# A decoder step on one core: the attention stage in another order of steps, with softmax scaling and weight splits on other engines

## The chip, the cores and the metric

The kernel runs on one core of a Trainium2 chip. The metric is the device time of one execution in microseconds (us). A core has five engines that matter here, each with its own in-order queue of instructions: TensorE (PE in the profile), VectorE (DVE), ScalarE (ACT), GpSimd (POOL) and SyncE (SP), which here only issues transfers. An instruction waits on semaphores for what other engines or transfers deliver, and whatever stands behind it on its engine waits too.

## The reference, cut to what matters

One layer of a decoder trunk runs over 256 prompt tokens and 8 samples of 4 new tokens, 288 columns in all. A first projection gives inputs of a recurrent branch, queries, three sets of keys and values, and gates; both branches are merged by gated projections; a convolutional feed-forward block follows. The changed stage computes the attention branch:

```python
def masked_softmax(s, mask):
    s = jnp.where(mask, s.astype(jnp.float32), NEG)
    e = jnp.where(mask, jnp.exp(s - jnp.max(s, axis=-1, keepdims=True)), 0.0)
    return e / jnp.maximum(jnp.sum(e, axis=-1, keepdims=True), 1e-30)
...
    g = jax.nn.sigmoid(g_nsa).reshape(B, T, 3, N_KV, HPG, 1)
    o = (g[:, :, 0] * o_cmp + g[:, :, 1] * o_slc + g[:, :, 2] * o_win).reshape(B, T, D_ATT)
    m = (jax.nn.sigmoid(g_m[..., :D_MODEL]) * (y_rnn @ w_proj_rnn)
         + jax.nn.sigmoid(g_m[..., D_MODEL:]) * (o @ w_proj_att))
```

There are three attentions (compressed, selected, window) over 8 heads in 2 groups. For the 256 prompt tokens all keys are on the chip; for each of the 8 samples 256 old keys and values of the selected and of the window branch come from memory. The kernel multiplies the gate of a branch into its softmax.

## The kernel before

All activations lie transposed, features on the 128 partitions and the 288 tokens along the free axis. Every weight product is made of three fp32r products (`mm3`): a weight tile of 128x1024 is loaded by SP, and split into a high part `wh` (a copy on ACT) and a low part `wl` (a difference, on DVE or POOL), by `split`; `load_w` issues the load and the split some tiles ahead of use. One tile is 24 matmuls over 288 columns, and that is a **step** of PE.

`run` walks through the steps of a stage and, after the matmuls of step n, calls the functions that `at(n, f, ...)` has put down for it. So a hand-written table of numbers sets the order in which instructions stand on every engine. The attention stage is `run([part_a(j) for j in range(KD)], side)`: 16 parts of three steps, 48 steps in all. In a part two steps make a gate (`th`, a product on DVE and a tanh on ACT) and one step multiplies the recurrent output (`yh`, `yl`) by `wpr` into `mA`. The attention work is the side work of these steps:

- A head and branch of the prompt: `h_score` (PE) with `soft0` (DVE: add the distance term, row maximum), then `soft1` (ACT: exp with sum), `soft2` (DVE: reciprocal of the sum, scaling), `h_turn` (PE transposes, ACT copies), `h_value` (PE).
- A sample's key or value tile `kt` of 128x512: `s_load` (SP), `s_parts0` (ACT: first bf16 part `k3`; POOL: the rest), `s_parts1` (ACT: second part; DVE: third part), then `s_key` or `s_value` (PE, 12 small bf16 matmuls). After four samples `s_key` reduces its two banks on DVE into `ss`.
- A sample group's softmax: `s_soft` or `s_cmp_soft`, `soft1`, `soft2`, `s_turn`, `s_turn1`.

The third part is line 176 (`V.tensor_sub(part(2), r, part(1))`), the rest of `s_parts0` line 859, the split lines 161 and 162, the scaling line 806. PSUM has eight banks by tag: two for weight products (`ps_g`), two for scores (`ps_s`), two for the samples' sums (`ps_b`), one each for transposes (`ps_t`) and a head's result (`ps_o`). The stage behind it (`part_b`) splits the attention result `q_sb` into `oh`, `ol` in its first step and uses them in its third.

The table of before, for the samples' tiles and the heads:

```python
    for b in range(NB):
        for n, kind, load, use, br in ((1, "k1", kslc, s_key, 1), (9, "k2", kwin, s_key, 2),
                                       (26, "v1", vslc, s_value, 1), (34, "v2", vwin, s_value, 2)):
            at(n + b, s_load, kind, load, b)
            at(n + b + 2, s_parts0, kind, b)
            at(n + b + 3, s_parts1, kind, b)
            at(n + b + 4, use, br, b)
```

Of the kernel before, what the change touches and what calls it, by code (L numbers as in the profile page):

```python
# [9 lines left out]
F32 = mybir.dt.float32  # L10
# [3 lines left out]
AF = mybir.ActivationFunctionType  # L14
ALU = mybir.AluOpType
# [3 lines left out]
P = 128  # L19
D = 2048  # L20
NP = 256
NB = 8
# [7 lines left out]
NG = 2  # L30
# [57 lines left out]
def body(ctx, tc, a, o):  # L88
    nc = tc.nc
    V, S, G, T = nc.vector, nc.scalar, nc.gpsimd, nc.tensor  # L90
# [13 lines left out]
    def pool(name, side="left", bufs=1):  # L104
        cm = tc.tile_pool(name=name, bufs=bufs, side=side, reuse_waits="tile")
        return cm, cm.__enter__()
# [5 lines left out]
    def w_tiles(src, shape=(8, P)):  # L112
        raw = wt.tile([P, *shape], F32, tag="raw", name="raw", bufs=4)
        if src is not None:
            nc.sync.dma_start(raw, src)
        return raw

    def w_parts(raw):
        shape = list(raw.shape)
        wh = wt.tile(shape, F32R, tag="wh", name="wh", bufs=3)  # L120
        wl = wt.tile(shape, F32R, tag="wl", name="wl", bufs=3)
        return wh, wl


    srcs = [a[w][j, i] for w, n in (("wxr", RB), ("wgr", RB), ("wq", NH), ("wks", 4), ("wkw", 4))
            for j in range(n) for i in range(2)]
    srcs += [a["wcm"][0, lh, k] for lh in range(2) for k in range(2)] + [a["wgn"]]
    GN = len(srcs) - 1
    srcs += [a["wcm"][1, lh, k] for lh in range(2) for k in range(2)]
    on_pool = set()  # L130
    for w, v in (("wga", "wpr"), ("wgb", "wpa")):
        for j in range(KD):
            srcs += [a[w][j, 0], a[w][j, 1], a[v][j]]
            if v == "wpr":
                on_pool.add(len(srcs) - 1)
    srcs += [a["wo"][j, i] for j in range(KD) for i in range(2)]
    for hf in range(2):
        for f in range(hf * FB // 2, (hf + 1) * FB // 2):
# [2 lines left out]
    raws, ready, at_ = [], [], [0]  # L141

    def load_w():
        i = at_[0]
        at_[0] += 1
        while len(ready) < min(i + 3, len(srcs)):
            while len(raws) < min(len(ready) + 4, len(srcs)):
                src = srcs[len(raws)]
                raws.append(w_tiles(src, src.shape[1:]))
            n = len(ready)  # L150
            if n == GN:
                w = wt.tile([P, KD, 64], F32R, tag="wh", name="wg2", bufs=3)
                V.memset(w[:, :, 24:32].bitcast(F32), 0.0)
                ready.append((w[:, :, 0:24], w[:, :, 32:56], w))
            else:
                ready.append(w_parts(raws[n]))
            split(*ready[n][:2], raws[n], G if n in on_pool else V)
        return ready[i]

    def split(hi, lo, src, eng=V):  # L160
        S.activation(hi, src, AF.Copy)  # L161
        eng.tensor_sub(lo, src, hi.bitcast(F32))  # L162
# [20 lines left out]
    def unit(out, n, xh, xl):  # L183

        for i in range(n):
            wh, wl = load_w()
            for k in range(8):
                kk = 8 * i + k
                mm3(out, wh[:, k], wl[:, k], xh[:, kk], xl[:, kk], kk == 0, kk == 8 * n - 1)
            if i < n - 1:  # L190
                yield
# [3 lines left out]
    def run(gens, side=None):  # L195

        n = 0
        for g in gens:
            old, late[:] = late[:], []
            for _ in g:  # L200
                for f in old:
                    f()
                old, late[:] = late[:], []
                for f in (side or {}).get(n, ()):
                    f()
                n += 1
            late[:] = old + late
# [83 lines left out]
    def x_load(c):  # L291
        xc = xp.tile([P, 2, N], F32, tag="xc", name="xc", bufs=8)
        raw = w_tiles(None)
        for ks in ((0, 1), (1, 2)) if c == 0 else ((0, 2),):
            nc.sync.dma_start(xc[:, ks[0]:ks[1]], a["x"][:, 2 * c + ks[0]:2 * c + ks[1]])
            first = c == 0 and ks[0] == 0
            (nc.scalar if first else nc.sync).dma_start(raw[:, 4 * ks[0]:4 * ks[1]], a["wkc"][c][:, 4 * ks[0]:4 * ks[1]])
            if first:
                nc.sync.dma_start(vec[:, V_GM:V_GM + KD], a["vec"][:, V_GM:V_GM + KD])
        if c == 5:  # L300
            nc.sync.dma_start(vec[:, KD:], a["vec"][:, KD:])
            nc.sync.dma_start(cs, a["cst"])
        return xc, raw
# [9 lines left out]
    for c in range(8):  # L313
        xc, raw = x_load(c)
# [3 lines left out]
        for k2 in range(2):  # L318
            k = 2 * c + k2
# [8 lines left out]
        for k2 in range(2):  # L328
            k = 2 * c + k2
# [74 lines left out]
    g = unit(qx[0][:, :N], 2, hh, hl)  # L404
# [9 lines left out]
    g = unit(qx[1][:, :N], 2, hh, hl)  # L414
# [117 lines left out]
    side = {}  # L532

    def at(n, f, *args):
        side.setdefault(n, []).append(lambda: f(*args))
# [91 lines left out]
    side = {}  # L627
# [18 lines left out]
    acm, ap = pool("ap")  # L646
# [60 lines left out]
    vs = ap.tile([NS, 2, NG, P], F32, name="vs")  # L707
# [75 lines left out]

    def soft0(key, sp, segs, nd, scale, gates):

        pr = ap.tile([P, 384], F32, tag="pr", name="pr", bufs=4)
        both = ap.tile([P, 4], F32, tag="mx", name="mx", bufs=4)
        mx, sm = both[:, 0:2], both[:, 2:4]
        for i, (s0, s1) in enumerate(segs):
            V.tensor_tensor_reduce(pr[:, s0:s1], sp[:, s0:s1], nd[:, s0:s1], 1.0, -3e38, op0=ALU.add, op1=ALU.max,  # L790
                                   accum_out=mx[:, i:i + 1])
        V.tensor_scalar(mx[:, :len(segs)], mx[:, :len(segs)], scale, -1.0, op0=ALU.mult, op1=ALU.mult)
        sx[key] = pr, mx, sm, segs, scale, gates
# [6 lines left out]
    def soft2(key):  # L800
        pr, mx, sm, segs, scale, gates = sx[key]
        n = len(segs)
        V.tensor_scalar(sm[:, :n], sm[:, :n], 1e-30, None, op0=ALU.max)  # L803
        V.reciprocal(sm[:, :n], sm[:, :n])
        for i, (s0, s1) in enumerate(segs):
            V.tensor_scalar(pr[:, s0:s1], pr[:, s0:s1], sm[:, i:i + 1], gates[:, i:i + 1], op0=ALU.mult, op1=ALU.mult)  # L806

    sx, pts, heads, pTs = {}, {}, {}, {}

# [39 lines left out]
        nc.sync.dma_start(t, a["wiv"][b])  # L849

    def s_load(kind, load, b):
        sx["raw", kind, b] = ap.tile([P, 2, NG, P], F32, tag="kt", name="kt", bufs=3)
        load(sx["raw", kind, b], b)

    def s_parts0(kind, b):
# [71 lines left out]
    def s_first():  # L927

        sx["o"] = [psb()[:, :384].rearrange("p (b x r) -> p b x r", b=NB, x=3) for _ in range(NG)]
        for g in range(NG):  # L930
            ot = sx["o"][g]
            T.matmul(ot[:, :, 0], vcs[:, g], pcT[:, g], start=True, stop=False, skip_group_check=True)
            for br in (1, 2):
                T.matmul(ot[:, :, 0], vs[:, br - 1, g], pts[br, g][1], start=False, stop=False, skip_group_check=True)

    def s_value(br, b):
        v3 = sx[f"v{br}", b][0]
# [13 lines left out]
                         so.rearrange("p b (h t) -> p b h t", t=TS))  # L951

    side = {}
    for b in range(NB):
        for n, kind, load, use, br in ((1, "k1", kslc, s_key, 1), (9, "k2", kwin, s_key, 2),
                                       (26, "v1", vslc, s_value, 1), (34, "v2", vwin, s_value, 2)):
            at(n + b, s_load, kind, load, b)
            at(n + b + 2, s_parts0, kind, b)
            at(n + b + 3, s_parts1, kind, b)
            at(n + b + 4, use, br, b)  # L960
    at(0, p_queries)
    at(0, p_values, 1, 0)
    at(1, p_values, 1, 1)
# [7 lines left out]
    at(3, p_cmp_copy)  # L971
    at(4, p_rows)
    at(5, p_cmp_exp)
    at(5, p_cmp_mask)
    at(6, p_cmp_values)
    at(7, p_cmp_norm)
    at(9, p_cmp_turn)
    at(13, s_cmp_turn)
    for i in range(2 * NH):
        n, h, br = 4 + int(i * 2.5), i // 2, 1 + i % 2  # L980
        at(n, h_score, h, br)
        at(n + 1, soft1, (h, br))
        at(n + 2, soft2, (h, br))
        at(n + 4, h_turn, h, br)
        at(n + 5, h_value, h, br)
    for g in range(NG):
        for n, key, first, last in ((13, ("p", 1, g), (s_soft, 1, g), (s_turn, 1, g)),
                                    (21, ("p", 2, g), (s_soft, 2, g), (s_turn, 2, g)),
                                    (9, ("c", g), (s_cmp_soft, g), None)):
            at(n + g, *first)  # L990
            at(n + g + 1, soft1, key)
            at(n + g + 2, soft2, key)
            if last:
                at(n + g + 4, *last)
                at(n + g + 5, s_turn1, *last[1:])
    side.setdefault(30, []).insert(0, s_first)
    at(46, s_last)
    run([part_a(j) for j in range(KD)], side)
    close(acm)
# [99 lines left out]
    g = unit(q0[:, :N], 2, h2h, h2l)  # L1099
# [8 lines left out]
    g = unit(q1[:, :N], 2, h2h, h2l)  # L1108
# [147 lines left out]
```

## Time and profile before

| | |
|---|---|
| median of 3 runs | 1673.66 us (1673.54 to 1673.69) |
| the profiled execution, its own time | 1674.1 us |
| its span, first to last instruction | 1672.3 us |
| PE busy | 1645.1 us, 98% |
| DVE busy | 1017.5 us, 61% |
| ACT busy | 765.3 us, 46% |
| POOL busy | 247.2 us, 15% |

Busy shares are means over stages with different limits. The profile also gives the granted clock of PE (1.00 is the full 2.4 GHz, 0.50 is 1.2 GHz), for each engine how long it stood idle and what released it, and the times of single instructions.

### The profile page before, as it was taken

Reading aid. Unit: us, or ns where it says so; the run is one execution under the profiler, and the core shown is the slowest. Engines: PE = TensorE matmul, PEld = TensorE weight load, DVE = VectorE, ACT = ScalarE, POOL = GpSimd, SP = SyncE. Lnnn points to the kernel's source line nnn. Section 1 sums busy time; section 2 is a strip of 40 time slices with the busy share of each in tenths; the row PEclk is TensorE's granted clock in tenths of the full one; section 3 lists DMA queues with packets and bytes.
Section 4 is the critical chain, followed back from the end, with each engine's and each line's share of the span. In section 5 each row is a group of like instructions: output and inputs, shape, how many; then the busy total and the mean of one; then the engine's idle time right before and its main releaser. Section 6 shows DMA issues by size and latency. Waiting matters only on the chain.

```text
span 1672.3 us, 31396 instructions
## 1 busy us (share of the span) xinstructions
PE 1645.1 (98%) x12722; PEld 1634.0 (98%) x12722; DVE 1017.5 (61%) x1544; ACT 765.3 (46%) x1091; POOL 247.2 (15%) x427
## 2 busy tenths in 40 slices
PE   9999999999999999999999999999999999999997
PEld 9999999899999999999999999999999999999997
DVE  6776867787775555666566556444456556654443
ACT  6555555565554444444444444333344444443332
POOL 0341100541440001330000000000000000001112
PEclk9999999999999999999999999999999999999999
DMA  7554585544556555555566655555555555555553
GB/s 269 178 170 132 156 295 175 157 144 153 171 169 212 164 174 167 167 169 159 172 200 205 198 163 167 172 171 165 167 163 165 175 163 166 174 175 175 157 175 107
DMA packets 88371, 290.79 MB, mean 174 GB/s; under 512 B 10178, under 2 KB 19154, under 8 KB 88098
## 3 DMA queue, kind: packets, MB, share of 16 engines
q1 hardware_dynamic: 85394, 276.73, 54.5%
q0 software_dynamic: 1968, 10.45, 1.9%
q8 instruction: 100, 1.64, 0.4%
q10 hardware_dynamic: 864, 1.59, 0.3%
q14 instruction: 45, 0.37, 0.1%
HBM read 284.02 MB, written 8.85 MB: 175 GB/s over the span
## 4 chain that ended last, share of the span: by engine, by line
PE 87%; DVE 6%; ACT 3%; issue 2%; POOL 1%; DMA 1%; SPq 0%; POOLq 0%; ACTq 0%; DVEq 0%
PE ps_g L179 28%; PE ps_g L181 27%; PE ps_g L180 27%; DVE wl L162 2%; PE ps_b L601 1%; DVE k L176 1%; ACT wh L161 1%; DVE mx L803 1%; DVE pr L806 1%; ACT pr L798 1%; DMA raw<-in_wkc_dram 0%; ACT k L175 0%; DVE pr L790 0%; POOL rest L859 0%; PE ps_b L181 0%
## 5 line engine op out<-in xcount | busy, mean ns | idle before, releaser
L162 DVE TENSOR_TENSOR wl<-raw,wh 128x1024 fp32r<-128x1024 f32 (+1 forms) x481 | 595.1, 1237 | 468.7 <-ACT wh L161 467.8
L161 ACT ACTIVATE wh<-raw 128x1024 fp32r<-128x1024 f32 (+1 forms) x497 | 523.4, 1053 | 362.7 <-PE ps_g L180 265.0
L179 PE MATMUL ps_g<-h2h,wh 128*128 128x288 f32 x1536 | 451.0, 294 | 0.0
L180 PE MATMUL ps_g<-h2l,wh 128*128 128x288 f32 x1536 | 450.8, 293 | 0.0
L181 PE MATMUL ps_g<-h2h,wl 128*128 128x288 f32 x1536 | 449.7, 293 | 0.0
L179 PE MATMUL ps_g<-hh,wh 128*128 128x288 f32 x1024 | 304.6, 297 | 1.2 <-DVE xr L375 0.7
L181 PE MATMUL ps_g<-hh,wl 128*128 128x288 f32 x1024 | 300.9, 294 | 4.3 <-DVE wl L162 4.3
L180 PE MATMUL ps_g<-hl,wh 128*128 128x288 f32 x1024 | 300.9, 294 | 0.0
L181 PEld LDWEIGHTS ps_g<-h2h,wl 128*128 128x128 f32 x1536 | 289.4, 188 | 0.0
L179 PEld LDWEIGHTS ps_g<-h2h,wh 128*128 128x128 f32 x1536 | 288.4, 188 | 0.1
L180 PEld LDWEIGHTS ps_g<-h2l,wh 128*128 128x128 f32 x1536 | 288.4, 188 | 0.1
L180 PE MATMUL ps_g<-gl,wh 128*128 128x288 f32 x768 | 225.4, 293 | 0.0
L179 PE MATMUL ps_g<-gh,wh 128*128 128x288 f32 x768 | 225.4, 293 | 0.0
L181 PE MATMUL ps_g<-gh,wl 128*128 128x288 f32 x768 | 224.8, 293 | 0.0
L181 PEld LDWEIGHTS ps_g<-hh,wl 128*128 128x128 f32 x1024 | 192.9, 188 | 5.9 <-DVE wl L162 5.9
L179 PEld LDWEIGHTS ps_g<-hh,wh 128*128 128x128 f32 x1024 | 192.4, 188 | 2.2 <-ACT wh L161 1.0
L180 PEld LDWEIGHTS ps_g<-hl,wh 128*128 128x128 f32 x1024 | 192.4, 188 | 0.2
L181 PEld LDWEIGHTS ps_g<-gh,wl 128*128 128x128 f32 x768 | 144.7, 188 | 0.0
L180 PEld LDWEIGHTS ps_g<-gl,wh 128*128 128x128 f32 x768 | 144.2, 188 | 0.0
L179 PEld LDWEIGHTS ps_g<-gh,wh 128*128 128x128 f32 x768 | 144.2, 188 | 0.0
L1065 POOL COPY fco<-u 128x2 f32<-128x2 f32 x48 | 8.8, 184 | 712.0 <-DVE u L1061 712.0
L1064 ACT ACTIVATE cv<-u,vec 128x304 f32<-128x304 f32 x48 | 30.8, 642 | 133.0 <-DVE u L1062 126.9
(328 smaller groups left out, 2101.6 us busy)
## 6 DMA issues: line engine op xcount, KB each, us to landing
raw<-in_wg_dram SPq DMA_DIRECT2D x96, 512.0 KB, 3.6
raw<-in_wu_dram SPq DMA_DIRECT2D x96, 512.0 KB, 4.1
raw<-in_wd_dram SPq DMA_DIRECT2D x96, 512.0 KB, 3.7
raw<-in_wga_dram SPq DMA_DIRECT2D x32, 512.0 KB, 3.6
raw<-in_wgb_dram SPq DMA_DIRECT2D x32, 512.0 KB, 3.6
raw<-in_wo_dram SPq DMA_DIRECT2D x32, 512.0 KB, 3.6
raw<-in_wxr_dram SPq DMA_DIRECT2D x16, 512.0 KB, 4.2
raw<-in_wgr_dram SPq DMA_DIRECT2D x16, 512.0 KB, 3.6
```

The costliest lines, as they stand in the source:

```text
L161: S.activation(hi, src, AF.Copy)
L162: eng.tensor_sub(lo, src, hi.bitcast(F32))
L176: V.tensor_sub(part(2), r, part(1))
L179: T.matmul(out, wh, xh, start=first, stop=False)
L180: T.matmul(out, wh, xl, start=False, stop=False)
L181: T.matmul(out, wl, xh, start=False, stop=last)
L601: T.matmul(pc[:, 2 * k:2 * k + 272], w[:, l], f(x), start=lh == 0 and k == 0 and l == 0 and n == 0, stop=lh == 1 and k == 1 and l == 7 and ...
L798: S.activation(pr[:, s0:s1], pr[:, s0:s1], AF.Exp, scale=scale, bias=mx[:, i:i + 1], accum_out=sm[:, i:i + 1])
L803: V.tensor_scalar(sm[:, :n], sm[:, :n], 1e-30, None, op0=ALU.max)
L806: V.tensor_scalar(pr[:, s0:s1], pr[:, s0:s1], sm[:, i:i + 1], gates[:, i:i + 1], op0=ALU.mult, op1=ALU.mult)
L1064: S.activation(cv[:, :FC], u[:, 2:2 + FC], AF.Identity, scale=vcol(V_FW + 96, f), bias=vcol(V_FB, f))
L1065: G.tensor_copy(fco[:, f, 0:2], u[:, NP:NP + 2])
```

## The change

It does five things. The table of the attention stage is written anew: a tile's load stands one step ahead of its first split part instead of two, its product two steps behind the second part instead of one, the key tiles get a free step after the fourth sample, sample softmaxes stand two steps apart, and within a step the products come first and the splits and loads last. The scaling of the softmax becomes a step of its own, `soft3`, on ACT; `soft2` multiplies the gate into the reciprocal instead. The low parts of the `wpr` tiles are made on DVE and no longer on POOL. `kt` has two buffers instead of three, `pr` and `mx` five instead of four. The samples' bias products are put down at two steps (`s_first`, `s_first2`).

```diff
-    on_pool = set()
     for w, v in (("wga", "wpr"), ("wgb", "wpa")):
         for j in range(KD):
             srcs += [a[w][j, 0], a[w][j, 1], a[v][j]]
-            if v == "wpr":
-                on_pool.add(len(srcs) - 1)
...
-            split(*ready[n][:2], raws[n], G if n in on_pool else V)
+            split(*ready[n][:2], raws[n])
...
-        pr = ap.tile([P, 384], F32, tag="pr", name="pr", bufs=4)
-        both = ap.tile([P, 4], F32, tag="mx", name="mx", bufs=4)
+        pr = ap.tile([P, 384], F32, tag="pr", name="pr", bufs=5)
+        both = ap.tile([P, 4], F32, tag="mx", name="mx", bufs=5)
...
         V.reciprocal(sm[:, :n], sm[:, :n])
+        V.tensor_mul(sm[:, :n], sm[:, :n], gates)
+
+    def soft3(key):
+        pr, mx, sm, segs, scale, gates = sx[key]
         for i, (s0, s1) in enumerate(segs):
-            V.tensor_scalar(pr[:, s0:s1], pr[:, s0:s1], sm[:, i:i + 1], gates[:, i:i + 1], op0=ALU.mult, op1=ALU.mult)
+            S.activation(pr[:, s0:s1], pr[:, s0:s1], AF.Copy, scale=sm[:, i:i + 1])
...
-        sx["raw", kind, b] = ap.tile([P, 2, NG, P], F32, tag="kt", name="kt", bufs=3)
+        sx["raw", kind, b] = ap.tile([P, 2, NG, P], F32, tag="kt", name="kt", bufs=2)
...
-            for br in (1, 2):
-                T.matmul(ot[:, :, 0], vs[:, br - 1, g], pts[br, g][1], start=False, stop=False, skip_group_check=True)
+            T.matmul(ot[:, :, 0], vs[:, 0, g], pts[1, g][1], start=False, stop=False, skip_group_check=True)
+
+    def s_first2():
+        for g in range(NG):
+            T.matmul(sx["o"][g][:, :, 0], vs[:, 1, g], pts[2, g][1], start=False, stop=False, skip_group_check=True)
...
-    for b in range(NB):
-        for n, kind, load, use, br in ((1, "k1", kslc, s_key, 1), (9, "k2", kwin, s_key, 2),
-                                       (26, "v1", vslc, s_value, 1), (34, "v2", vwin, s_value, 2)):
-            at(n + b, s_load, kind, load, b)
-            at(n + b + 2, s_parts0, kind, b)
-            at(n + b + 3, s_parts1, kind, b)
-            at(n + b + 4, use, br, b)
...
+    for br, kind, load, n in ((1, "k1", kslc, 1), (2, "k2", kwin, 11), (1, "v1", vslc, 26), (2, "v2", vwin, 34)):
+        for b in range(NB):
+            m = n + b + (b // 4 if kind[0] == "k" else 0)
+            at(m + 5, s_key if kind[0] == "k" else s_value, br, b)
     for i in range(2 * NH):
         n, h, br = 4 + int(i * 2.5), i // 2, 1 + i % 2
         at(n, h_score, h, br)
         at(n + 1, soft1, (h, br))
         at(n + 2, soft2, (h, br))
-        at(n + 4, h_turn, h, br)
-        at(n + 5, h_value, h, br)
+        at(n + 3, soft3, (h, br))
+        at(n + 5, h_turn, h, br)
+        at(n + 6, h_value, h, br)
...
     side.setdefault(30, []).insert(0, s_first)
+    side.setdefault(38, []).insert(0, s_first2)
+    for br, kind, load, n in ((1, "k1", kslc, 1), (2, "k2", kwin, 11), (1, "v1", vslc, 26), (2, "v2", vwin, 34)):
+        for b in range(NB):
+            m = n + b + (b // 4 if kind[0] == "k" else 0)
+            at(m + 3, s_parts1, kind, b)
+            at(m + 2, s_parts0, kind, b)
+            at(m + 1, s_load, kind, load, b)
```

How the rows of an engine move is shown at three places. The first is DVE in step 6 of the stage, which finishes the first softmax, begins the second and makes the third part of sample 2 (`k_3801` before, `k_3787` after; `pr`, `mx` belong to a softmax, `ISA` is the addition with a row maximum and the reading of that maximum). Before:

```order
L176 TENSOR_TENSOR k_3801<-rest,k_3801 128x512
L803 TENSOR_SCALAR mx<-mx 128x2
L804 RECIPROCAL mx<-mx 128x2
L806 TENSOR_SCALAR pr<-pr,mx,gts 128x128
L806 TENSOR_SCALAR pr<-pr,mx,gts 128x256
L790 ISA pr,mx<-ps_s,cs 128x128
L790 ISA mx 128x1
L790 ISA pr,mx<-ps_s,cs 128x256
L790 ISA mx 128x1
L792 TENSOR_SCALAR mx<-mx 128x2
L162 TENSOR_TENSOR wl<-raw,wh 128x1024
```

And with the change:

```order
L800 TENSOR_SCALAR mx<-mx 128x2
L801 RECIPROCAL mx<-mx 128x2
L802 TENSOR_TENSOR mx<-mx,gts 128x2
L787 ISA pr,mx<-ps_s,cs 128x128
L787 ISA mx 128x1
L787 ISA pr,mx<-ps_s,cs 128x256
L787 ISA mx 128x1
L789 TENSOR_SCALAR mx<-mx 128x2
L173 TENSOR_TENSOR k_3787<-rest,k_3787 128x512
L159 TENSOR_TENSOR wl<-raw,wh 128x1024
```

The two scalings of `pr` are gone, a product of 128x2 with the gates has come, and the sample's part has moved to the end of the step. Its product on PE stands in step 7 before, in step 8 after.

The second place is POOL from step 5 to step 10: `rest` is the difference of a sample's tile, `wl` the low part of a weight tile, `vcp` and `pcs` belong to the compressed branch. Before:

```order
L768 TENSOR_TENSOR pcs<-pcs,cs 128x128 x2
L162 TENSOR_TENSOR wl<-raw,wh 128x1024
L859 TENSOR_TENSOR rest<-kt,k_3858 128x512
L734 TENSOR_TENSOR vcp<-vc,cs 128x1024
L859 TENSOR_TENSOR rest<-kt,k_3932 128x512
L776 TENSOR_TENSOR pcs<-pcs,t_3474 128x128 x2
L859 TENSOR_TENSOR rest<-kt,k_3996 128x512
L162 TENSOR_TENSOR wl<-raw,wh 128x1024
L859 TENSOR_TENSOR rest<-kt,k_4062 128x512
```

And with the change:

```order
L765 TENSOR_TENSOR pcs<-pcs,cs 128x128 x2
L731 TENSOR_TENSOR vcp<-vc,cs 128x1024
L860 TENSOR_TENSOR rest<-kt,k_3862 128x512
L773 TENSOR_TENSOR pcs<-pcs,t_3474 128x128 x2
L860 TENSOR_TENSOR rest<-kt,k_3986 128x512
L860 TENSOR_TENSOR rest<-kt,k_4061 128x512
```

The weight splits are gone from this queue, here and further on.

The third place is ACT in steps 6 and 7: `wh` is a weight tile's high part, `k<-kt` and `k<-rest` a sample's first and second part, `th` the tanh of the gate. Before:

```order
L161 ACTIVATE wh<-raw 128x1024
L175 ACTIVATE k_3801<-rest 128x512
L173 ACTIVATE k_3858<-kt 128x512
L733 ACTIVATE vc<-ps_s 128x128
L736 ACTIVATE vcs<-ps_s 128x256
L161 ACTIVATE wh<-raw 128x1024
L654 ACTIVATE th<-th 128x288
L175 ACTIVATE k_3858<-rest 128x512
L173 ACTIVATE k_3932<-kt 128x512
L798 ACTIVATE pr,mx<-pr,mx 128x128
L798 ACTIVATE pr,mx<-pr,mx 128x256
```

And with the change:

```order
L158 ACTIVATE wh<-raw 128x1024
L730 ACTIVATE vc<-ps_s 128x128
L733 ACTIVATE vcs<-ps_s 128x256
L172 ACTIVATE k_3787<-rest 128x512
L170 ACTIVATE k_3862<-kt 128x512
L158 ACTIVATE wh<-raw 128x1024
L651 ACTIVATE th<-th 128x288
L807 ACTIVATE pr<-pr,mx 128x128
L807 ACTIVATE pr<-pr,mx 128x256
L795 ACTIVATE pr,mx<-pr,mx 128x128
L795 ACTIVATE pr,mx<-pr,mx 128x256
L172 ACTIVATE k_3862<-rest 128x512
```

The sample's parts stand behind the softmax work of their step, the two scalings (line 807) have come, and after the fourth sample (`k_3862`) no new tile begins in step 7.

## Rows read from the trace of the kernel before

**Rows 1.** The page, part 1: busy time, share of the span, instructions.

```profile
PE 1645.1 (98%) x12722; PEld 1634.0 (98%) x12722; DVE 1017.5 (61%) x1544; ACT 765.3 (46%) x1091; POOL 247.2 (15%) x427
```

**Rows 2.** Busy time by stretches of the attention stage, and their sum; PEclk: granted clock.

```profile
core 0: us, PE busy (x) PEld busy (x) DVE busy (x) ACT busy (x) POOL busy (x), PEclk, DMA share, GB/s
...
322.00:332.00 10.00, 8.88 (x86) 8.53 (x85) 9.76 (x22) 5.67 (x9) 7.11 (x6) 1.00 0.59 174
...
346.00:350.00 4.00, 3.24 (x24) 2.89 (x24) 3.09 (x8) 1.62 (x3) 0.00 (x0) 0.62 0.32 73
...
sum 212.00, PE 204.04 PEld 197.62 DVE 160.43 ACT 123.38 POOL 87.81; mean PE 9.72 PEld 9.41 DVE 7.64 ACT 5.88 POOL 4.18
```

**Rows 3.** PE's waits, 290 to 502: total us, times, longest us.

```profile
PE ps_b L941 <- DVE k L176: 2.5, 3, 1.5
PE ps_b L878 <- DVE k L176: 1.9, 3, 1.1
PE ps_b L878 <- DVE ss L882: 1.9, 1, 1.9
PE ps_b L878 <- ACT k L175: 1.5, 1, 1.5
```

**Rows 4.** DVE's timeline: start us, duration us, instruction.

```profile
326.29 2.33 DVE L803 TENSOR_SCALAR mx<-mx 128x2 f32<-128x2 f32 x1
...
340.78 3.32 DVE L806 TENSOR_SCALAR pr<-pr,mx,gts 128x128 f32<-128x128 f32 x2
```

**Rows 5.** POOL's timeline at the same places.

```profile
325.77 2.82 POOL L162 TENSOR_TENSOR wl<-raw,wh 128x1024 fp32r<-128x1024 f32 x1
...
340.44 2.39 POOL L162 TENSOR_TENSOR wl<-raw,wh 128x1024 fp32r<-128x1024 f32 x1 [0.53 <-ACT wh L161]
```

**Rows 6.** POOL's groups, 290 to 502: busy us, mean ns, idle before.

```profile
L859 POOL TENSOR_TENSOR rest<-kt,k 128x512 f32<-128x512 f32 x32 | 39.6, 1239 | 68.3 <-ACT k L173 61.4 <-issue 4.3 <-PE ps_g L180 1.3
L162 POOL TENSOR_TENSOR wl<-raw,wh 128x1024 fp32r<-128x1024 f32 x15 | 37.9, 2523 | 49.4 <-ACT wh L161 49.4
```

**Rows 7.** DVE's groups, 290 to 502.

```profile
L162 DVE TENSOR_TENSOR wl<-raw,wh 128x1024 fp32r<-128x1024 f32 x32 | 39.9, 1246 | 20.0 <-ACT wh L161 19.9
L176 DVE TENSOR_TENSOR k<-rest,k 128x512 bf16<-128x512 f32 x32 | 36.6, 1144 | 14.7 <-ACT k L175 14.6
L806 DVE TENSOR_SCALAR pr<-pr,mx,gts 128x128 f32<-128x128 f32 (+1 forms) x32 | 19.3, 644 | 0.6
L803 DVE TENSOR_SCALAR mx<-mx 128x2 f32<-128x2 f32 (+1 forms) x22 | 16.5, 750 | 0.0
...
L792 DVE TENSOR_SCALAR mx<-mx 128x2 f32<-128x2 f32 x16 | 6.6, 415 | 0.6
L806 DVE TENSOR_SCALAR pr<-pr,mx,gs 128x288 f32<-128x288 f32 (+1 forms) x6 | 4.3, 722 | 0.2
...
L804 DVE RECIPROCAL mx<-mx 128x2 f32<-128x2 f32 (+1 forms) x22 | 3.6, 165 | 0.8
```

**Rows 8.** Two lines of DVE: shortest, median, longest in ns; first and last start.

```profile
L176 DVE TENSOR_TENSOR k<-rest,k x32: 679/693/2524, 304.5 to 488.5; 128x512 bf16<-128x512 f32 x32
...
L792 DVE TENSOR_SCALAR mx<-mx x16: 168/170/1697, 306.0 to 479.6; 128x2 f32<-128x2 f32 x16
```

**Rows 9.** ACT's groups, 290 to 502.

```profile
L173 ACT ACTIVATE k<-kt 128x512 bf16<-128x512 f32 x32 | 19.7, 615 | 0.0
...
L823 ACT ACTIVATE pT<-ps_t 128x384 f32<-128x384 f32 x16 | 7.7, 481 | 14.0 <-PE ps_t L821 14.0
...
L782 ACT ACTIVATE pct<-ps_s 128x256 f32<-128x256 f32 x1 | 0.4, 383 | 0.1
...
L733 ACT ACTIVATE vc<-ps_s 128x128 f32<-128x128 f32 x1 | 0.3, 277 | 2.1 <-DVE k L176 2.1
```

**Rows 10.** The tile kt: its loads, from issue to landing.

```profile
DMA to landing us min/median/max: 2.0/3.3/5.5
```

**Rows 11.** DVE's timeline at the end of the stage.

```profile
501.49 3.03 DVE L162 TENSOR_TENSOR ol<-q_sb,oh 128x288 fp32r<-128x288 f32 x8
```

**Rows 12.** PE's timeline, the first product that uses this result.

```profile
505.45 0.29 PE L179 MATMUL ps_g<-oh,wh 128*128 128x288 f32 x1
```

More of the change, by code (lines that the diff above doesn't have):

```diff
@@ L973, in body @@
     at(5, p_cmp_exp)
-    at(5, p_cmp_mask)
+    at(6, p_cmp_mask)
     at(6, p_cmp_values)
-    at(7, p_cmp_norm)
-    at(9, p_cmp_turn)
-    at(13, s_cmp_turn)
+    at(8, p_cmp_norm)
+    at(10, p_cmp_turn)
+    for br, kind, load, n in ((1, "k1", kslc, 1), (2, "k2", kwin, 11), (1, "v1", vslc, 26), (2, "v2", vwin, 34)):
+        for b in range(NB):
+            m = n + b + (b // 4 if kind[0] == "k" else 0)
+            at(m + 5, s_key if kind[0] == "k" else s_value, br, b)
     for i in range(2 * NH):
@@ L983, in body @@
         at(n + 2, soft2, (h, br))
-        at(n + 4, h_turn, h, br)
-        at(n + 5, h_value, h, br)
+        at(n + 3, soft3, (h, br))
+        at(n + 5, h_turn, h, br)
+        at(n + 6, h_value, h, br)
     for g in range(NG):
[L987 to L992, printed above, removed]
+        for n, key, first, last in ((15 + 2 * g, ("p", 1, g), (s_soft, 1, g), (s_turn, 1, g)),
+                                    (25 + 2 * g, ("p", 2, g), (s_soft, 2, g), (s_turn, 2, g)),
+                                    (7 + g, ("c", g), (s_cmp_soft, g), None)):
+            at(n, *first)
+            at(n + 1, soft1, key)
+            at(n + 2, soft2, key)
+            at(n + 3, soft3, key)
             if last:
-                at(n + g + 4, *last)
-                at(n + g + 5, s_turn1, *last[1:])
+                at(n + 5, *last)
+                at(n + 6, s_turn1, *last[1:])
+    at(12, s_cmp_turn)
     side.setdefault(30, []).insert(0, s_first)
+    side.setdefault(38, []).insert(0, s_first2)
[5 more added lines that the diff above has]
+            at(m + 1, s_load, kind, load, b)
     at(46, s_last)
```

## The prediction

> **What bounds the kernel now.** I read the page first: TensorE (PE) is busy in 1645.1 of 1672.3 us [rows 1], so a change can only win what PE idles, or what it does at a lower clock. Then I cut the changed stage into stretches. The attention stage fills 290 to 502 us; in those 212.0 us PE is busy in 204.04 [rows 2], so 7.96 us of PE time are idle here. VectorE (DVE) is busy in 160.4 us of the same stretch, but unevenly: in 322 to 332 us it is busy in 9.76 of 10 us, and PE loses 1.1 us there. Third, PE's own waits in the stage: all but 0.2 us of the 7.96 is in four rows, and these name two lines only, 878 (the key products of a sample) and 941 (its value products), which wait for the last piece of the three-way split of a key or value tile (DVE line 176, or ACT line 175 ahead of it) or for the reduction that frees the score banks (line 882); the longest single wait is 1.9 us [rows 3]. No wait for a weight split stands among them. One more loss hides behind a wait: in 346 to 350 us the granted clock is 0.62 [rows 2], a mean over a piece at 1.2 GHz and a piece at 2.4, after PE had stood still for 1.9 us. PE was busy in 3.24 us there, so about 3.24 x 0.38 = 1.2 us would not be needed at the full clock.
>
> So PE waits because DVE is late, and the next view says why it is late. DVE's timeline shows a tiny operation on 128x2 elements (line 803) that starts at 326.29 and takes 2.33 us, and two scalings (line 806) that start at 340.78 and take 3.32 us together [rows 4]. GpSimd (POOL) runs a weight split over 128x1024 from 325.77 for 2.82 us and from 340.44 for 2.39 us [rows 5]: the small operation ends within 0.03 us of the POOL instruction's end. Whole groups say the same: line 176 has a median of 0.69 us and a mean of 1.14, line 792 a median of 0.17 and a mean of 0.42 [rows 7, 8]. With the median as the undisturbed time, line 176 loses 36.6 - 32 x 0.69 = 14.5 us, line 792 6.6 - 16 x 0.17 = 3.9, and line 803, set against the reciprocal on the same tile (0.165 us), 16.5 - 22 x 0.165 = 12.9 [rows 7]. That is 31.3 us of standing still in DVE's 160.4. Line 162, DVE's own weight split, loses nearly nothing (mean 1.246).
>
> **The change part by part.**
>
> *Weight splits from POOL to DVE.* Sixteen subtractions leave POOL, which took 2.52 us for one [rows 6], and cost DVE 16 x 1.246 = 19.9 us [rows 7]. POOL's remaining work in the stage is 87.8 - 37.9 = 49.9 us [rows 2, 6], nearly all of it the 32 differences of line 859. The stalls above came from these two kinds of POOL work, 37.9 and 39.6 us long; I take half of the 31.3 us as gone, with nothing and all as the two ends.
>
> *Scaling from DVE to ACT.* The 38 scalings of line 806 leave DVE, 19.3 + 4.3 = 23.6 us [rows 7]. What stays is one product of 128x2 for each of 22 softmaxes; the nearest row is the reciprocal of the same tile, so 22 x 0.165 = 3.6 us. ACT gains 38 copies with a scale. The trace has none from SBUF in this form, so I go by ACT's copies of like width, 0.277 us for 128 columns, 0.383 for 256, and 0.481 for 384 as the upper end for 288 [rows 9]: 18 x 0.277 + 16 x 0.383 + 4 x 0.481 = 13.0 us. ACT's busy time goes from 123.4 [rows 2] to 136.4 of some 203 us, 67%; it is hidden in ACT's idle time, and without that cover it would be 13.0 us on the path.
>
> DVE's sum: 160.4 - 23.6 + 19.9 + 3.6 - 15.6 = 144.7 us, with ends 129.0 and 160.3. Of a stage of 203 us that is 71% (64% to 79%); it was 76%. DVE does not become the bound by its mean, though it does one weight split more in every third step.
>
> The Trainium skill, page "SBUF — State Buffer", section "Who interferes with whom", says that DVE and GpSimd share one pair of ports, that the second to issue blocks until the first is done, and that a DVE instruction with two SBUF inputs contends with a GpSimd instruction that reads SBUF. The rows above agree for lines 803, 806 and 176. By this rule the sixteen moved subtractions, which have two SBUF inputs, can be held by a line 859 difference too, which speaks against this part of the change. By the row the 32 such splits that DVE already has are held for hardly anything. By the rule at its worst, 16 x 1.24 = 19.8 us more on DVE, its sum would be 164.5; by the row it stays at 144.7. That is the second rival below.
>
> *Order of steps.* A step is one weight tile of PE, 212/48 = 4.4 us. Before, a sample's second split stage ran one step ahead of the product that uses it; now two. The eight waits of these rows, at most 1.9 us each, are shorter than the step gained, so all of lines 878 and 941 should go, with about 2.5 us to spare. The first key group's reduction now has a free step before the banks are used again (the extra step after the fourth sample), which takes away the 1.9 us wait on line 882. Both softmax chains keep their distance from the transposition: it waits for the scaling two steps earlier, as before. With fewer operations that use a score bank in one step (two at most, three before) no new wait for a bank is seen. Without idle stretches of 1.9 us the clock should stay at its upper level, so the 1.2 us come back too.
>
> *New waits.* The first split of sample b+3 writes the buffer that the product of sample b reads, and now both stand in the same step, so ACT waits there for PE. Behind it on ACT stands the next weight split, which PE wants two steps later; ACT's mean load of 136.4/48 = 2.8 us a step leaves 1.4 us a step to catch up. The raw tile now has two buffers and is loaded one step ahead instead of two; SP queues the next weight load behind it. One buffer's round is ACT's copy, 0.62 us, POOL's difference, 1.24, and 3.3 (at most 5.5) from the issue to the landing [rows 6, 9, 10]: 5.2 to 7.4 us against two steps of the shorter stage, 8.5 us. It holds, with 1.1 us left at the upper end, so it costs nothing. The last head's value product moves from the stage's step 46 to 47. Before, the last output split of DVE starts with its group at 501.49, runs 3.03 us, and PE's first product that uses it starts at 505.45 [rows 11, 12], so 0.9 us were to spare; the move takes about half of it. I put 0 to 1.0 us on this edge. The bias products split over two places are the same eight, and cost nothing new.
>
> *Sum.* Against the profiled execution's 1674.1 us (span 1672.3 and 1.8 around it): -8.0 (waits), -1.2 (clock), +0.6 (edge and small leftovers, from the 0 to 1.0 and one wait of 0.2) = 1665.5. That execution lies 0.44 above the median of the runs, 1673.66, so the time forecast is **1665.1 us**. Nothing left over would be 1664.5.
>
> **The rivals.**
> 1. *Forecast*: both causes go, 1665.1 (1664.0 to 1667.0). Chance 0.72.
> 2. *DVE fills up again.* The stalls move from the scalings to the added weight splits, DVE's sum stays near 160, and in the stretches where it was busy 9.76 of 10 us it is late by more than a step, so that th, the mixer product or a weight split is late next. Half of the 9.2 us would stay: 1673.7 - 4.6 = 1669.1. For it: the stretch at 322 us. Against: those stretches were full because of POOL's 2.4 us blocks. Chance 0.14.
> 3. *Nothing changes.* What PE waits for is late by the chain ACT-POOL-ACT-DVE and not by its distance, and ACT's in-order wait for PE eats the added step: 1673.7. Against: even in 322 to 332 us ACT is busy in 5.67 and POOL in 7.11 of 10 us [rows 2]. Chance 0.08.
> 4. *Slower: the raw tile becomes the bound.* If a landing takes more than 8.5 - 0.62 - 1.24 = 6.6 us on the mean, each pair of tiles stretches two steps; 16 pairs at 1 us over it cost 16 us against the 9.2 won, so 1673.7 - 9.2 + 16 = 1680.5. It turns slower from 0.6 us over it, a landing of 7.2. For it: one buffer less, a weight tile of 512 KB in flight beside each load. Against: 3.3 median and 5.5 at most now [rows 10]. Chance 0.06.
>
> **How the numbers follow.** A measurement of this kernel can tell about 0.2%, 3.3 us, from no change, so faster means below 1670.3. The forecast and most of the second rival lie there: 0.72 + 0.13 = 0.85. Same: 0.08 and the rest of the second, 0.09. Slower: 0.06. The range goes from 1663.8, the floor of 1664.5 less the uncertainty of the clock term, to 1669.8, which takes in the second rival's centre; outside stay the two last cases and the upper tail of the second, some 0.16.
>
> **What would show it.** Right: in the stage PE's idle falls from 8.0 to below 1.5 us; the waits at the two lines of key and value products are gone; the granted clock is 1.00 all through; the DVE groups of the small scalings and of the three-way split have means near their medians; POOL shows no weight split in this stage; DVE's busy time is near 145 us, ACT's near 136. Wrong: PE waits for a weight split or for th, a wait of ACT for a DMA of the raw tile, or a weight split on DVE with a mean well over 1.25 us.

## The result, and the profile after

The kernel with the change takes 1664.37 us (median; 1663.64 to 1665.39) beside 1673.68 for the kernel before in the same measurement: a ratio of 0.9944 with an interval of 0.9932 to 0.9956, 9.3 us faster. The forecast was 1665.1. The profiled execution took 1663.64 us, with a span of 1661.9; it lies among the quickest of its kernel, so it shows 10.5 us less than the one of before.

The page of the kernel after, busy time, share of the span and instructions of each engine:

```profile
PE 1642.5 (99%) x12722; PEld 1631.8 (98%) x12722; DVE 994.7 (60%) x1544; ACT 777.4 (47%) x1129; POOL 206.8 (12%) x411
```

PE idles 1661.9 - 1642.5 = 19.4 us; before it was 27.2 [rows 1]. Nothing else of PE's work has changed. Stretches of the attention stage after, same columns as [rows 2], and below them PE's waits in the stage (total, times, longest):

```profile
322.00:332.00 10.00, 9.89 (x93) 9.45 (x92) 9.57 (x27) 5.79 (x13) 3.06 (x4) 1.00 0.54 161
...
346.00:350.00 4.00, 4.00 (x33) 3.95 (x31) 3.96 (x11) 3.60 (x9) 1.24 (x2) 1.00 0.70 187
...
sum 202.00, PE 201.31 PEld 195.13 DVE 138.56 ACT 135.22 POOL 49.26; mean PE 9.59 PEld 9.29 DVE 6.60 ACT 6.44 POOL 2.35
```

```profile
PE ps_o L831 <- ACT pT L824: 0.5, 1, 0.5
```

PE's idle time in the stage fell from 7.96 us to 0.69, and both lines of [rows 3] are gone from its waits. The granted clock of 346 to 350 us was 0.62 and is 1.00. The stretch at 322 us is worth a look: DVE is busy in 9.57 of 10 us there, hardly less than before (9.76), and yet PE loses 0.1 us instead of 1.1. A full engine costs nothing as long as nobody is waiting at that moment for what it makes.

DVE's groups after, 290 to 492 us, as [rows 7]:

```profile
L159 DVE TENSOR_TENSOR wl<-raw,wh 128x1024 fp32r<-128x1024 f32 x47 | 64.4, 1372 | 25.8 <-ACT wh L158 25.7
L173 DVE TENSOR_TENSOR k<-rest,k 128x512 bf16<-128x512 f32 x32 | 22.9, 715 | 19.1 <-ACT k L172 19.0
...
L789 DVE TENSOR_SCALAR mx<-mx 128x2 f32<-128x2 f32 x16 | 5.9, 370 | 0.6
L800 DVE TENSOR_SCALAR mx<-mx 128x2 f32<-128x2 f32 (+1 forms) x22 | 4.6, 208 | 0.0
...
L802 DVE TENSOR_TENSOR mx<-mx,gts 128x2 f32<-128x2 f32 x16 | 3.4, 212 | 0.5
```

The groups whose stalls were added up before have almost their undisturbed means: 22.9 - 32 x 0.69 = 0.8 us of standing still on line 173, 4.6 - 22 x 0.165 = 1.0 on line 800, 5.9 - 16 x 0.17 = 3.2 on line 789, 5.0 in all instead of 31.3. Weight splits, however, went from a mean of 1246 ns to 1372, which is 64.4 - 47 x 1.246 = 5.8 us. Two timelines show where it comes from; the first is DVE's, the second POOL's at the same place (start, duration, instruction):

```profile
322.12 1.23 DVE L159 TENSOR_TENSOR wl<-raw,wh 128x1024 fp32r<-128x1024 f32 x1 [0.26 <-ACT wh L158]
...
325.62 2.17 DVE L159 TENSOR_TENSOR wl<-raw,wh 128x1024 fp32r<-128x1024 f32 x1
```

```profile
325.55 1.17 POOL L860 TENSOR_TENSOR rest<-kt,k 128x512 f32<-128x512 f32 x1
```

The same split takes 1.23 us alone and 2.17 where a difference on POOL began 0.07 us before it: 0.94 more, out of the 1.10 that POOL still had to run. That is what the Trainium skill, page "SBUF — State Buffer", section "Who interferes with whom", says of a DVE instruction with two SBUF inputs against a GpSimd instruction that reads SBUF, and the trace agrees. In this stage 23 of the 47 splits begin while such a difference runs, most of them near its end: fifteen take 1.33 to 1.35 us, eight take 1.55 to 2.18. In the kernel before one of 32 began with more than 0.1 us of a difference still to run, and that one took 2.03 us.

ACT's scalings after, and POOL's only large group:

```profile
L807 ACT ACTIVATE pr<-pr,mx 128x128 f32<-128x128 f32 (+2 forms) x38 | 15.6, 451 | 1.1 <-DVE mx L802 0.9
```

```profile
L860 POOL TENSOR_TENSOR rest<-kt,k 128x512 f32<-128x512 f32 x32 | 38.7, 1208 | 123.2 <-ACT k L170 103.4 <-DVE k L173 12.8 <-DVE mx L787 2.2
```

### The profile page after: what moved, and what is told of

Read it like the earlier page. It is cut to its first block, busy times and chain, and to the rows that moved or that the text cites. A ratio compares the mean times of both kernels' runs of the same rounds, so it can differ in the third digit from the quotient of the medians.

```text
span 1661.9 us, 31421 instructions
## 1 busy us (share of the span) xinstructions
PE 1642.5 (99%) x12722; PEld 1631.8 (98%) x12722; DVE 994.7 (60%) x1544; ACT 777.4 (47%) x1129; POOL 206.8 (12%) x411
## 4 chain that ended last, share of the span: by engine, by line
PE 94%; DVE 2%; ACT 2%; issue 1%; POOL 0%; DMA 0%; SPq 0%; POOLq 0%; ACTq 0%; DVEq 0%
PE ps_g L176 29%; PE ps_g L178 29%; PE ps_g L177 29%; PE ps_b L598 1%; DVE wl L159 1%; ACT wh L158 1%; PE ps_o L831 0%; DMA raw<-in_wkc_dram 0%; PE ps_s L816 0%; PE ps_t L822 0%; PE ps_b L945 0%; PE ps_b L178 0%; POOL x L1160 0%; DVE C L507 0%; PE ps_b L176 0%
## 5 line engine op out<-in xcount | busy, mean ns | idle before, releaser
L159 DVE TENSOR_TENSOR wl<-raw,wh 128x1024 fp32r<-128x1024 f32 (+1 forms) x497 | 621.1, 1250 | 473.9 <-ACT wh L158 471.6
```

## The experiments

The theory to test: PE waited because POOL's long weight splits held DVE up, and a sample's product stood too close behind its last split part; engines and order both act, and either covers part of the other. The main rival: one of the pieces alone (the distance, or the moved splits) does all of it and the rest is ornament. A second: the two raw tile buffers nearly bound the stage. Each kernel has a ratio to the kernel before, taken on the same chip; us are the difference of the two medians there. Ratios have intervals of about 0.001 (2 us) on each side.

**The three parts apart.** e1_splits is the kernel before with one line of the change:

```diff
-            split(*ready[n][:2], raws[n], G if n in on_pool else V)
+            split(*ready[n][:2], raws[n])
```

> The kernel before, with only the sixteen low parts of the wpr tiles moved from POOL to DVE; order of steps and scaling as before. Two theories of the 9.3 us. Margin theory: PE waits because the samples' split parts stand one step ahead of their product, and the order is the cure; then this run keeps most of the waits, PE idle in the attention stage 5 to 8 us, time 1670 to 1674. Stall theory: PE waits because POOL's 2.4 us splits hold DVE; then this run wins most, PE idle 1 to 3 us, time 1665.5 to 1668. Both expect the means of DVE's small scalings (line 803 before) to fall to near 0.2 to 0.4 us.

Measured: 1667.38 us, 0.9958 (0.9944 to 0.9971), 6.3 us faster. PE's waits in the attention stage, and two of DVE's groups:

```profile
PE ps_b L878 <- DVE k L176: 1.9, 3, 1.1
PE ps_b L878 <- ACT k L175: 0.6, 1, 0.6
PE ps_s L924 <- DVE pr L806: 0.2, 1, 0.2
PE ps_b L878 <- DVE mx L803: 0.2, 1, 0.2
```

```profile
L176 DVE TENSOR_TENSOR k<-rest,k 128x512 bf16<-128x512 f32 x32 | 29.8, 933 | 10.4 <-ACT k L175 10.3
...
L803 DVE TENSOR_SCALAR mx<-mx 128x2 f32<-128x2 f32 (+1 forms) x22 | 7.0, 319 | 0.0
...
L792 DVE TENSOR_SCALAR mx<-mx 128x2 f32<-128x2 f32 x16 | 5.9, 367 | 0.6
```

The time lies in the range of the stall theory. DVE has sixteen weight splits more to do, and PE waits 2.9 us instead of 8.0: the tiny line 803 went from a mean of 750 ns to 319, and the wait for line 882 and those at line 941 are gone. Reckoned as in the prediction, the three groups stand still for 7.7 + 3.4 + 3.2 = 14.3 us, so the moved splits alone take away 17.0 of 31.3. The price of a block on POOL is not its own work but what stands still behind it on DVE. Another way for the same move to act would be that a sample's difference stands behind a long split in POOL's own queue; but ACT waits for these differences (`rest`) 1.6 us in four places in the kernel before and 1.6 us in four places here.

e3_order has only the new table of steps (and the buffers): splits on POOL as before, scaling on DVE in `soft2`.

```diff
-            split(*ready[n][:2], raws[n])
+            split(*ready[n][:2], raws[n], G if n in on_pool else V)
...
-        at(n + 3, soft3, (h, br))
```

> The changed kernel's order of steps alone; wpr low parts on POOL and scaling on DVE as before. Margin theory: the eight waits are covered although DVE is held as much as before (some 31 us), PE idle below 2 us, 1664.5 to 1666.5. Stall theory: DVE is late by more than the step gained in places, PE idle 3 to 6 us, 1668 to 1671.

Measured: 1666.72 us, 0.9958 (0.9944 to 0.9971), 6.9 us faster. PE's waits in the stage, and two of DVE's groups:

```profile
PE ps_g L179 <- DVE th L653: 1.5, 1, 1.5
PE ps_b L878 <- DVE k L176: 1.1, 1, 1.1
PE ps_g L181 <- POOL wl L162: 0.8, 1, 0.8
```

```profile
L162 DVE TENSOR_TENSOR wl<-raw,wh 128x1024 fp32r<-128x1024 f32 x31 | 44.4, 1431 | 16.1 <-ACT wh L161 16.1
L806 DVE TENSOR_SCALAR pr<-pr,mx,gts 128x128 f32<-128x128 f32 (+1 forms) x32 | 26.6, 873 | 0.6
```

The opposite picture at nearly the same time, which lies between the two ranges. DVE stands still as much as before, at other lines: the three groups lose 17.2 us instead of 31.3, but line 806 takes 8.6 more (873 ns against 644 [rows 7]), and the weight splits lose 44.4 - 31 x 1.246 = 5.8. DVE is busy for 1016.5 us of the span, before for 1017.5. But the waits fall to 3.4 us, and they are of other kinds: the gate `th`, and a weight split that POOL itself brings too late. The order hides the blocks; it does not remove them.

e2_scale and e4_splits_scale put the scaling on ACT in the old order, in the step after `soft2`, alone and together with e1's line:

```diff
+        at(n + 3, soft3, (h, br))
...
+            at(n + g + 3, soft3, key)
```

> The kernel before, with only the scaling of the softmax moved from DVE to ACT one step later (the transposition stays where it was); POOL still makes the wpr low parts. Margin theory: 1671 to 1674. Stall theory: DVE loses 23.6 us of work that POOL could hold, but the holds move to the next operation that POOL can hold (the split's third part, the small scalings), so 1669 to 1672, PE idle 4 to 6 us.

> The kernel before with the splits on DVE and the scaling on ACT, in the old order of steps. Margin theory: half of the waits or more stay, 1668 to 1672. Stall theory: as good as the whole change, 1664.5 to 1666.5, PE idle below 2 us.

Measured: e2_scale 1675.83 us, 1.0009 (1.0000 to 1.0018); e4_splits_scale 1668.57, 0.9968 (0.9955 to 0.9980). Both carry a fault of their own: with one step more in the compressed softmax chain, the last group's scaling and the transposition that reads it (`s_cmp_turn`) fall into the same step. PE waits for it 3.0 us in e2_scale and 2.9 in e4_splits_scale. So these two say nothing of the scaling's worth, except that the added step needs room in the table; e2_scale is above both of its ranges. e10_scale and e11_splits_scale give it that room by starting this chain one step earlier:

```diff
-                                    (9, ("c", g), (s_cmp_soft, g), None)):
+                                    (8, ("c", g), (s_cmp_soft, g), None)):
```

> The scaling on ACT alone, again, with the compressed branch's softmax begun one step earlier, so that its scaling stands a step ahead of its transposition (in the first run of this kind it stood in the same step, and PE waited 3.0 us there). If the loss of that run was this one wait, this run is at 1671 to 1674; if moving the scaling to ACT in the old order makes the samples' chain later, 1674.5 to 1677.

> Splits on DVE and scaling on ACT in the old order, with the same correction. If the scaling has a worth of its own beside the splits, 1664.5 to 1666.5 (below the 1667.4 of the splits alone); if it has none, 1666.5 to 1668.

Measured: e10_scale 1671.89 us, 0.9987 (0.9978 to 0.9996), 2.5 us faster (0.7 to 3.7 by the interval); e11_splits_scale 1665.04, 0.9945 (0.9932 to 0.9959), 9.4 us faster, which nothing here tells from the whole change. PE's only wait in the stage of e11_splits_scale:

```profile
PE ps_b L882 <- DVE k L176: 1.2, 2, 0.9
```

The two moves between engines give the whole gain in the old order, with the old distance of one step and the old buffers (only the compressed softmax begins a step earlier). What made PE wait was a DVE that came late, not the distance as such.

**The new order with a part taken back.** e5_order_scale is the kernel after with the `wpr` splits on POOL again, e6_order_splits the kernel after with the scaling on DVE again (diffs as in e3_order, one half each).

> The changed kernel with the wpr low parts back on POOL. Margin theory: within 1 us of the changed kernel, 1664 to 1665.5, although DVE's held time comes back in part. Stall theory: 1666 to 1669.

> The changed kernel with the scaling back on DVE. Margin theory: within 1 us of the changed kernel, 1664 to 1665.5. Stall theory: 23.6 us more on DVE and the holds by line 860 on them, 1665 to 1668.

Measured: 1666.36 us, 0.9954 (0.9940 to 0.9967), 7.3 us faster than before; and 1665.05, 0.9948 (0.9934 to 0.9961), 8.6 us faster. Against the whole change's 9.3, taking back the splits costs 2 us and the scaling 0.7, about as much as the intervals. In e5_order_scale PE waits for POOL's split itself, and one of DVE's smallest operations pays for the blocks:

```profile
PE ps_g L181 <- POOL wl L162: 1.4, 1, 1.4
```

```profile
L805 DVE TENSOR_TENSOR mx<-mx,gts 128x2 f32<-128x2 f32 x16 | 14.9, 933 | 0.5
```

**The distance by itself.** e7_near takes the added step away in the new order, e12_margin adds it in the old one (and shifts the samples' softmaxes by the same step). e7_near:

```diff
-            at(m + 5, s_key if kind[0] == "k" else s_value, br, b)
+            at(m + 4, s_key if kind[0] == "k" else s_value, br, b)
```

and e12_margin, on the kernel before:

```diff
-            at(n + b + 4, use, br, b)
+            at(n + b + 5, use, br, b)
...
-        for n, key, first, last in ((13, ("p", 1, g), (s_soft, 1, g), (s_turn, 1, g)),
-                                    (21, ("p", 2, g), (s_soft, 2, g), (s_turn, 2, g)),
+        for n, key, first, last in ((14, ("p", 1, g), (s_soft, 1, g), (s_turn, 1, g)),
+                                    (22, ("p", 2, g), (s_soft, 2, g), (s_turn, 2, g)),
```

> The changed kernel with the samples' products one step nearer to their second split part (one step ahead again, all else as changed). Margin theory: the splits now also stand last in a step, so the waits on the third part come back, 3 to 8 us of PE idle, 1667 to 1672. Stall theory: DVE is no longer held by POOL's long splits, so few waits come back, below 2 us, 1664 to 1666.

> The kernel before with one change: every sample product one step later (two steps behind its second split part), and the sample softmaxes one step later with them. Engines, order within a step, loads and buffers as before. If the step gained is what the new order gives, 1665 to 1668, with PE idle below 3.5 us in the attention stage; if it is the place within the step, the free step after the fourth sample or the spread of the softmaxes, 1669 to 1673.

Measured: e7_near 1673.00 us, 0.9993 (0.9984 to 1.0002); e12_margin 1672.97, 0.9992 (0.9983 to 1.0001). Neither can be told from the kernel before. PE's waits in the stage, e7_near first:

```profile
PE ps_b L879 <- DVE k L173: 3.0, 6, 1.0
PE ps_b L945 <- DVE k L173: 1.2, 3, 0.5
PE ps_b L879 <- ACT k L172: 1.1, 1, 1.1
```

```profile
PE ps_s L924 <- DVE pr L806: 2.0, 2, 1.1
PE ps_o L830 <- ACT pT L823: 1.8, 1, 1.8
PE ps_s L915 <- ACT pct L782: 1.4, 1, 1.4
PE ps_s L781 <- POOL pcs L776: 1.1, 1, 1.1
PE ps_g L179 <- DVE th L653: 0.4, 1, 0.4
PE ps_s L898 <- DVE rest L906: 0.3, 1, 0.3
PE ps_b L878 <- DVE ss L882: 0.2, 1, 0.2
```

In e7_near DVE is hardly held up at these parts any more (line 173 has a mean of 698 ns), and PE still waits 5.3 us for them, with a time above both ranges: in the new order they stand last in their step, so that the step of distance is needed. In e12_margin that wait is gone, and 7.2 us of others have come. DVE is held as before (line 176 has a mean of 1100 ns, before 1144; line 803 has 697, before 750), and PE stands still in the same places: from 312 to 332 us for 2.9 us, before 3.2, and from 342 to 350 us for 2.0, as before. The next user of what comes late waits in the sample's place. A step of distance for one user moves the stall to the next one.

**The raw tile.** e8_one_raw gives `kt` one buffer:

```diff
-        sx["raw", kind, b] = ap.tile([P, 2, NG, P], F32, tag="kt", name="kt", bufs=2)
+        sx["raw", kind, b] = ap.tile([P, 2, NG, P], F32, tag="kt", name="kt", bufs=1)
```

> The changed kernel with one buffer for the raw sample tile instead of two: the fourth rival's mechanism, made to act. A buffer's round of 0.62 + 1.2 + 3.3 = 5.1 us now has one step of 4.2 us, so each of 32 tiles would come 0.9 us late: 1680 to 1694, with PE waiting for the samples' parts. If most of the landing time is queueing that a later issue does not meet, or the two steps of margin take it up, 1664.5 to 1670.

Measured: 1674.93 us, 1.0004 (0.9993 to 1.0014), so 10 us slower than with two buffers (by the two ratios). ACT's waits for the raw tile in the stage:

```profile
ACT k L170 <- DMA kt<-in_slk_dram: 10.1, 5, 3.4
ACT k L170 <- DMA kt<-in_wiv_dram: 8.6, 6, 2.1
ACT k L170 <- DMA kt<-in_slv_dram: 7.4, 5, 2.3
ACT k L170 <- DMA kt<-in_wik_dram: 5.9, 4, 1.9
```

ACT stands still for 32.0 us, 20 times; PE waits 7.6 us in the stage, not for a sample but above all for `th` (2.3), weight splits (1.7) and the transposed rows (1.4). The late copy holds up what stands behind it on ACT, and so DVE, which waits 47.7 us for ACT's high parts instead of 25.8. The mechanism of the fourth rival exists, at a price between the two ranges of this run; one reason is that a landing takes 2.3 us (median) here, and not the 3.3 reckoned with. With two buffers the trace shows no wait of ACT for this tile, and landings of 3.3 us (median) and 4.9 (longest).

**The same idea elsewhere.** The longest row of PE's waits in the kernel after, as in the one before, is in the recurrent stage, 150 to 190 us. There one step's `r_scan0` ends in an ACT instruction (line 504) that waits for a DVE result begun in the same step, and the next weight tile stands behind it on ACT:

```profile
ACT B L504 <- DVE A L502: 17.3, 7, 2.6
```

In e9_scan it becomes a step of its own, and the scan follows one step later:

```diff
         V.tensor_mul(A[:, j, :RC], A[:, j, :RC], C[:, j, :RC])
+
+    def r_scan_b(j):
         S.activation(B[:, j, :RC], B[:, j, :RC], AF.Identity, scale=2.0, bias=mone)
...
-        at(29 + j, r_scan1, j)
+        at(29 + j, r_scan_b, j)
+        at(30 + j, r_scan1, j)
```

> The changed kernel, with the same rule used in the recurrent stage: ACT's B = 2B - 1 of a block stands one step behind the DVE products that free it, and the scan one step further. In the changed kernel PE waits there 4.3 us in seven places for a low weight part, in a ring of ACT weight copy, DVE low part, DVE scan and products, ACT B. If the ring is the cause, these waits go and the time is 1659.5 to 1661; if DVE's load is (9 of 10 us busy in the later stretches), they stay, 1663.5 to 1665.

Measured: 1656.72 us, 0.9900 (0.9885 to 0.9915), 7.65 us below the change (7.4 by the two ratios), quicker than either kernel, and 2.8 us below its range. PE's wait in the kernel after that is gone in e9_scan, then the stretch of 150 to 190 us of the kernel after, then the same of e9_scan:

```profile
PE ps_g L178 <- DVE wl L159: 4.3, 7, 0.7
```

```profile
150.00:190.00 40.00, 35.23 (x252) 33.12 (x251) 28.43 (x51) 19.03 (x25) 4.58 (x9) 1.00 0.44 128
```

```profile
150.00:190.00 40.00, 40.00 (x307) 40.00 (x307) 36.17 (x73) 22.29 (x32) 5.82 (x13) 1.00 0.59 170
```

PE idled 4.77 us there, yet it does 55 matmuls more in the same 40 us, which at 40.00 / 307 = 0.130 us is 7.2 us. PE's timeline of the kernel after tells why a stall costs more than the idle time shown for it:

```profile
159.73 0.29 PE L177 MATMUL ps_g<-hl,wh 128*128 128x288 f32 x1
159.86 0.29 PE L178 MATMUL ps_g<-hh,wl 128*128 128x288 f32 x1
160.66 0.40 PE L176 MATMUL ps_g<-hh,wh 128*128 128x288 f32 x1 [0.50 <-ACT wh L158]
160.89 0.30 PE L177 MATMUL ps_g<-hl,wh 128*128 128x288 f32 x1
161.91 0.40 PE L178 MATMUL ps_g<-hh,wl 128*128 128x288 f32 x1 [0.73 <-DVE wl L159]
```

Starts are 0.13 us apart in a running row, but each matmul is listed with 0.29. From 159.86 to 160.66 it is 0.80, so 0.67 is lost where the wait says 0.50; and the next start, at 160.89, comes 0.23 later instead of 0.13. Each stall hides about 0.17 + 0.10 = 0.27 us beside its wait, 8 stalls 2.2 us: 4.8 + 2.2 = 7.0, close to the 7.2 and to the 7.65 measured.

## Why the prediction was right, step by step

- **What bounds the kernel.** Right: only PE's idle time and its clock were to be won. Of the profiled execution's 10.5 us, 7.8 are idle time (27.2 - 19.4; the forecast was 8.0 - 0.6 = 7.4). The other 2.6 are PE's own busy time, 1645.1 - 1642.5, for the same 12722 instructions. The clock is some 1.7 of them and not 1.2: the 0.62 is a mean over 4 us in which PE also stood still, and PE was at work nearly all of the time at 0.50 (2.93 us from 347 to 350), and at 0.81 in the microsecond after it. The 0.9 left over was not in the sum. It may be the hidden part of a stall; at the 0.27 us found in the recurrent stage the 8 stalls that went would hide 2.2, but the products that wait here are smaller, and no run shows their price. So the profiled execution came out 1.9 us under the 1665.5 forecast for it. That the median is only 0.7 under its forecast is partly luck: the profiled execution is the quickest of four, 0.7 under their median, and the one of before lay 0.4 above its own.
- **Weight splits from POOL to DVE.** The direction and the mechanism were right, and e1_splits shows them by themselves. Half of the 31.3 us was taken as gone; 17.0 went with the moved splits alone, 26.3 with the whole change. In turn the weight splits now lose 5.8 us; I had put that at nothing and its worst at 19.8. The row that I took for it, 32 splits of DVE held for hardly anything, showed only that they seldom met a difference on POOL. And it is not the move that changes this but the new order: in the old order DVE's splits have a mean of 1275 ns (e1_splits) and 1267 (e11_splits_scale), in the new one between 1337 (e6_order_splits) and 1458 (e5_order_scale). DVE's sum is 138.6 us instead of 144.7, inside the ends of 129.0 and 160.3.
- **Scaling to ACT.** The 38 scalings fill 15.6 us instead of 13.0: ACT's exponentials of the same shapes (393 and 496 ns before) were the nearer rows, not its copies; the scalings took 394 and 498. ACT's sum is 135.2, forecast 136.4, which is partly luck, since neighbours on ACT are listed some 0.1 us into each other and the sum grew by 11.8 only. The cover held. The scaling is worth 2.5 us where DVE is short (e10_scale), and less than can be measured where it isn't (e6_order_splits against the change).
- **Order of steps.** The conclusion held, the reason didn't: "The eight waits of these rows, at most 1.9 us each, are shorter than the step gained, so all of lines 878 and 941 should go, with about 2.5 us to spare." They go, in e12_margin too but for 0.2 us, but there the stall comes back at other lines and nothing is won. And e11_splits_scale wins all of it without any new distance. I had treated a wait as a property of the line that waits; it belonged to the engine that was late.
- **New waits.** No wait for the raw tile, none of note for ACT's earlier write of a sample's buffer, and the stage's end costs nothing visible. What is left over is one wait of 0.5 us, in the 0 to 1.0 I had put there, though at another line (the transposed rows).
- **The rivals.** DVE filling up again is real as a mechanism and far too small to decide. "Nothing changes" fails with the 7.3 us of idle time that went in the stage. The raw tile decides with one buffer, not with two.

So the two remedies overlap: engines alone 9.4 us, order alone 6.9, both 9.3. The rival that one piece does all is refuted for the distance. For the moved splits alone (6.3 of 9.3 us) the traces speak against it, with 2.9 us of waits left instead of 0.5; the times don't settle it, for the intervals of the two ratios overlap from 0.9944 to 0.9956. Still open is what in the new order, beside the distance, gives e3_order its 6.9 us (the place of the splits at the end of a step, the free step after the fourth sample, the softmaxes two steps apart, a head's transposition one step later, the window keys two steps later): these weren't run apart.

## What to carry to other kernels

When several lines wait for one late engine, find what holds that engine up before giving its users more room: a step of distance for one user passes the stall to the next (e12_margin), while taking long work off the neighbour that blocks it eases the stalls of all of them at once (e1_splits, PE's waits from 8.0 to 2.9 us). Where work is put into steps for engines that run in order, an instruction that waits for a result of its own step holds up everything behind it; a step of its own for it (e9_scan) brought 7.65 us, where this whole change brought 9.3. Price a stall by starts, or by counting instructions in a fixed stretch, not by the idle time alone.

## What was unexpected of the hardware

- An operation's size says little of how long it can be held: on 128x2 elements DVE's product with two inputs takes 212 ns on the mean beside POOL's 1.2 us differences, and 933 ns when POOL also runs splits of 2.4 us (e5_order_scale, at most 2241); alone it takes 160 to 190 ns.
- A matmul of 288 columns after a stall takes 0.10 us more to its successor (0.23 to 0.24 instead of 0.13, at five stalls between 160 and 175 us of the kernel after), and the granted clock is 1.00 there.
